# Attention scores of a hybrid decoder layer: key tiles of 288 columns, low keys on 128 rows, a PSUM bank for each query head

## The chip, the core and the metric

The kernel runs on one core of a Trainium2 chip. The time is the device time of one execution in microseconds; the comparison is between medians of several executions. TensorE (PE in the profile) multiplies matrices: a weight load (LDWEIGHTS, row PEld) puts up to 128 x 128 numbers into its array, a matmul streams the other operand through and adds into PSUM, a memory of eight banks of 512 fp32 columns for each of 128 partitions. VectorE (DVE), ScalarE (ACT) and GpSimd (POOL) do the elementwise work, SyncE (SP) issues most transfers.

## The reference

One layer of a trunk for a prompt of 2048 tokens and a sample group of 32 tokens, all in fp32. What matters here is the banded attention of the prompt:

```python
qb = q.reshape(B, nb, BLOCK, N_KV_HEADS, GROUP, HEAD_DIM)          # blocks of 128 queries
kb = jnp.concatenate([kp[:, :-1], kp[:, 1:]], axis=2)              # 256 keys: block before and own
s = jnp.einsum('bnqkgd,bnskd->bnkgqs', qb, kb) * scale
mask = (rel >= 0) & (rel < WINDOW) & (kpos[:, None, :] >= 0)
probs = sink_softmax(s, mask, sink)                                # softmax with a sink per head
o = jnp.einsum('bnkgqs,bnskd->bnqkgd', probs, vb)
```

There are 8 query heads of 64 dimensions and 2 key/value heads, so a key/value head serves four query heads. Around it stand the norms, the input projection, a convolution branch of 31 taps, the merge with two gates, the output projection and the SwiGLU.

## The kernel before

**Precision.** Weights and activations are split into a high part in fp32r and a low part (the fp32 value less the high part), and a product is three fp32r matmuls: high x high, high x low, low x high. All GEMMs are built this way, 24 matmuls for a tile of 128 outputs by one chunk of tokens.

**Stages.** The tokens form two groups: group 0 of 1024 prompt tokens in chunks of 512, group 1 of the other 1024 and the 32 sample tokens in chunks of 352. Each group goes through the input projection (`mixer_in`), the merge and output projection (`mixer_out`) and the feed-forward part (`ffn`).

**Order of work.** The program is written out by hand; each engine executes its instructions in the order in which they are issued. The GEMMs form the main stream. After each GEMM tile, `gemm_group` calls `pump`, which keeps running totals of the estimated TensorE and VectorE time (`Timed`, `pe_cost`, `dve_cost`). When a step of the attention is due (every 4200 ns of estimated TensorE time) it issues one step of `attn_gen`; then it issues convolution taps (`dw`, 1024 columns each on VectorE) as long as VectorE's total is less than 1400 ns ahead. In group 0 the units of the adaLN conditioning (`ada_unit`, tiles `wh`,`wl` by `cs`) stand between the GEMMs as well; four of them share one PSUM bank, which they hold until the result is turned.

**The attention of a block of 128 queries** takes four steps, one after each of four GEMM tiles:
- A: the probabilities of the previous block's second key/value head are transposed, the values of its first head are multiplied (`attn_pv`, PSUM tile from `mm()`, evacuated by two ScalarE copies `oa` and `ob`), then `attn_scores` for key/value head 0;
- B: the probabilities of head 0 are normalised on GpSimd, `attn_pv` for the previous block's second head, then `attn_scores` for head 1;
- C: head 1 is normalised, the block's values are transposed (`v_block`);
- D: head 0's probabilities are transposed, and the next block's keys and queries are stacked (`k_stack`, `q_stack`).

`attn_scores` is called 32 times, twice for each of 16 blocks. The stacked queries `qst` hold, for each query head, the high part on the 64 rows of its key/value head and the low part on the other 64. The high keys `kh` stand twice over the 128 rows, so one matmul of 128 rows gives (high + low query) x high key; a second one on the 64 rows of the high queries gives high query x low key. The keys are a ring of two blocks of 128 columns, 256 in all. Two query heads share a PSUM bank. VectorE then adds the mask and takes the maximum (the `CUSTOM_DVE_ANT_0` rows `p<-ps,mask`), ScalarE takes the exponentials.

**PSUM and buffers.** Of the eight banks, four belong to the GEMM pool (`mm()`), two to `ps()`, two to `pt()`. A pool gives out the bank that was freed longest ago, and the first matmul into it waits for its last reader. A bank is freed when the program drops the tile: the bank of a GEMM tile only when the next one is taken, so during an attention step the bank of the GEMM just finished is still held. Temporary tiles (`tmp`, pool `tmpp`) rotate through 13 buffers of 2 KB per partition, two of which hold `kh` and `kl` while an attention runs.

Of the kernel before, what the change touches and what calls it, by code (L numbers as in the profile page):

```python
# [10 lines left out]
F32 = mybir.dt.float32  # L11
F32R = mybir.dt.float32r
# [26 lines left out]
]  # L39
SLOT = 1056  # L40

VROWS = [("b_ada", 48), ("norm1_g", 8), ("norm2_g", 8), ("conv_b", 4), ("conv_ln_g", 4), ("conv_ln_b", 4)]
# [35 lines left out]
class Timed:  # L78
    """An engine whose instructions add their estimated length to a running total."""

# [40 lines left out]
class Builder:  # L121
    def __init__(self, ctx, tc, a, o):
        self.tc, self.nc, self.a, self.o = tc, tc.nc, a, o
        self.V = Timed(self.nc.vector, dve_cost)
        self.T = Timed(self.nc.tensor, pe_cost)
        P = bass.MemoryType.PSUM
        self.big = ctx.enter_context(tc.tile_pool(name="big", bufs=30))
        self.tmpp = ctx.enter_context(tc.tile_pool(name="tmpp", bufs=13))
        self.wrp = ctx.enter_context(tc.tile_pool(name="wrp", bufs=2))
        self.wpp = ctx.enter_context(tc.tile_pool(name="wpp", bufs=4))  # L130
        self.const = ctx.enter_context(tc.tile_pool(name="const", bufs=1))
        self.small = ctx.enter_context(tc.tile_pool(name="small", bufs=2))
        self.pmm = ctx.enter_context(tc.tile_pool(name="pmm", bufs=4, space=P))
        self.pss = ctx.enter_context(tc.tile_pool(name="pss", bufs=2, space=P))
        self.ptt = ctx.enter_context(tc.tile_pool(name="ptt", bufs=2, space=P))
        self.xT_d = [[self.dram(f"xT{g}_{f}", (128, GROUPS[g]["w"])) for f in range(KD)] for g in range(2)]
        self.gate_d = [[self.dram(f"gate{g}_{m}", (128, GROUPS[g]["w"])) for m in range(16)] for g in range(2)]
        self.tasks = []
        self.soon = []
        self.task_t = 0.0  # L140
        self.task_dt = 4200
        self.bg = []
        self.plan = []
        self.raws, self.units = [], []
# [18 lines left out]

# [1 line left out]
    def add_unit(self, key, fill):  # L165
# [169 lines left out]

# [1 line left out]
    def step(self, gens, i=0):  # L337
        """Advance a generator; None when it wants to wait for the next step."""
        try:
            return next(gens[i])  # L340
        except StopIteration:
            gens.pop(i)
            return 1

    def pump(self, slack=1400, lag=3500):
        """A step of the attention when one is due, and as much of the other side work as VectorE has time for."""
        if self.tasks and self.T.t >= self.task_t:
            self.task_t = max(self.task_t, self.T.t - 3000) + self.task_dt
            self.step(self.tasks)
        self.V.t = max(self.V.t, self.T.t - lag)  # L350
        i = 0
        while i < len(self.soon):
            if self.step(self.soon, i) is None:
                i += 1
        i = 0
        while i < len(self.bg) and self.V.t < self.T.t + slack:
            if self.step(self.bg, i) is None:
                i += 1
# [14 lines left out]

# [1 line left out]
    def gemm(self, ps, cw, terms, hi_first=False):  # L375
# [18 lines left out]
    def gemm_group(self, keys, act, g, evac, hi_first=False, ready=None):  # L394
        """GEMMs of several weight tiles, all of them on one chunk of tokens before the next chunk."""
        units = [self.w_next(k) for k in keys]
        evs = [evac(k) for k in keys]
        chunks = GROUPS[g]["chunks"]
        for n, (c0, cw) in enumerate(chunks):
            while ready is not None and ready() < c0 + cw:  # L400
                self.step(self.bg)
            for u, ev in zip(units, evs):
                ps = self.gemm_tile(u, act, c0, cw, hi_first=hi_first)
                ev(ps, c0, cw)
                self.pump()
                if n == len(chunks) - 1:
                    self.w_done()
# [11 lines left out]

# [1 line left out]
    def params_load(self):  # L421
# [49 lines left out]
    def params2(self):  # L471
# [19 lines left out]
        nc.gpsimd.memset(self.kg[:, :128], 0.0)  # L491
        self.us = c.tile([128, KC, NS], F32, name="us")
        self.vz = []
        for i in range(3):
# [57 lines left out]

# [1 line left out]
    def tok_tiles(self, g, c0, cw):  # L554
# [178 lines left out]

# [1 line left out]
    def in_evac(self, key):  # L735
        """Returns the function that takes one finished chunk of this tile of the input projection."""
        nc = self.nc
# [105 lines left out]

# [1 line left out]
    def hist_raws(self):  # L845
# [129 lines left out]
    def rstd_bcast(self, g, sm, c0, cw, ones, eps):  # L975
        """(mean over features of sm + eps) ** -0.5 for a chunk's tokens, on all partitions."""
        nc = self.nc
# [18 lines left out]

# [1 line left out]
    def vz_write(self, z, src):  # L998
        """A block's values, for kv head 0 as [hi | lo] and for kv head 1 as [lo | hi]."""
        for v in range(2):  # L1000
# [16 lines left out]
    def k_stack(self, n, bi):  # L1017
        """The keys of a block into their half of the ring: hi twice over the partitions for each kv head, lo once."""
        nc, R = self.nc, self.ROWS
        src = self.kg[:, (n + 1) * 128:(n + 2) * 128]  # L1020
        half = (bi + 1) % 2
        for kv in range(2):
            for r in range(2):
                nc.scalar.activation(out=self.kh[R[r], kv, half], in_=src[R[kv]], func=AF.Copy)
            nc.gpsimd.tensor_tensor(out=self.kl[R[kv], half], in0=src[R[kv]], in1=self.kh[R[kv], kv, half].bitcast(F32), op=ALU.subtract)

    def q_stack(self, n, kv):
        """A kv head's four query heads of a block: hi on the head's own partitions, lo on the others."""
        nc, r, o = self.nc, self.ROWS[kv], self.ROWS[1 - kv]
# [7 lines left out]
    def attn_scores(self, qs, kv, mask):  # L1037
        nc = self.nc
        r = self.ROWS[kv]
        mx = self.small.tile([128, 4], F32, tag="mx", name="mx")  # L1040
        es = self.small.tile([128, 4], F32, tag="es", name="es")
        den = self.small.tile([128, 4], F32, tag="den", name="den")
        P = []
        for jp in range(2):
            ps = self.ps()
            p = self.tmp("p")
            P += [p[:, :256], p[:, 256:]]
            for e in range(2):
                j = jp * 2 + e
                out = ps[:, e * 256:e * 256 + 256]  # L1050
                self.T.matmul(out, qs[:, j], self.kh[:, kv].rearrange("p h t -> p (h t)"), start=True, stop=False)
                self.T.matmul(out, qs[r, j], self.kl[r].rearrange("p h t -> p (h t)"), start=False, stop=True)
            for e in range(2):
                j = jp * 2 + e
                self.V.tensor_tensor_reduce(out=P[j], in0=ps[:, e * 256:e * 256 + 256], in1=mask,
                                               scale=1.0, scalar=-3e38, op0=ALU.add, op1=ALU.max, accum_out=mx[:, j:j + 1])
        sink = self.sink[:, kv * 4:kv * 4 + 4]
# [40 lines left out]
    def attn_gen(self, g):  # L1098
# [8 lines left out]
        prev = None  # L1107
        self.kh = self.tmp("kh", dt=F32R).rearrange("p (v h t) -> p v h t", v=2, h=2)
        self.kl = self.tmp("kl", 256, dt=F32R).rearrange("p (h t) -> p h t", h=2)
        self.k_stack(-1, g * 8 - 1)  # L1110
# [16 lines left out]
        for n in range(8):  # L1127
# [25 lines left out]
            yield 0  # L1153
        self.kh = self.kl = None
        pv_first()
# [105 lines left out]

# [1 line left out]
    def split(self, src, W, name, eng=None):  # L1263
# [131 lines left out]

# [1 line left out]
    def norm2(self, g):  # L1397
# [140 lines left out]
    def boot(self):  # L1538
        """From the inputs to the first four tiles of group 0's input projection, ahead of the steady stream."""
        nc = self.nc  # L1540
# [116 lines left out]

# [1 line left out]
    def program(self):  # L1659
# [59 lines left out]
```

## Time and profile before

| what | value |
| --- | --- |
| median of 3 runs | 2974.28 us (2974.13 to 2978.0) |
| span of the profiled execution | 2973.9 us, 0.4 us below the median |
| busy share PE, PEld, DVE, ACT, POOL | 96%, 85%, 48%, 30%, 37% |
| score matmuls of 128 rows | 128, mean 390 ns |
| score matmuls of 64 rows | 128, mean 412 ns |
| mask passes on VectorE | 128, mean 419 ns |

The span of the profile is the profiled execution's own time; it goes from the first to the last instruction. A row of the timeline has start, duration, engine, line, operation and tiles; the bracket at its end gives the idle time of the engine before it and what ended it. All instructions recorded through the two `Timed` engines have line 89, so groups are told apart by their tiles. Matmuls overlap in the records: the pace of a stream is read from one start to the next, not from a duration.

### The profile page before, as it was taken

How to read it: one execution, taken by the hardware profiler on the slowest of the kernel's cores; microseconds unless marked ns; L12 is line 12 of the kernel's file. 1: busy time of each engine (PE TensorE's matmuls, PEld its weight loads, DVE VectorE, ACT ScalarE, POOL GpSimd, SP SyncE). 2: the span in 40 equal slices, each digit the busy share in tenths (PEclk: the TensorE clock that was granted, in tenths of full speed). 3: DMA queues.
4: the chain of work that ended last, by engine and by line, in shares of the span. 5: the costliest groups of instructions: out<-in, count | busy, mean ns of one | idle time of the engine just before them, and what ended most of it. 6: DMA issues, size and time to landing. Idle time of an engine off the chain costs nothing. (4 is left out here: it accounts for less than half of the span.)

```text
span 2973.9 us, 37568 instructions
## 1 busy us (share of the span) xinstructions
PE 2869.8 (96%) x14852; PEld 2513.0 (85%) x14852; DVE 1426.2 (48%) x2376; ACT 894.0 (30%) x1763; POOL 1098.4 (37%) x810
## 2 busy tenths in 40 slices
PE   8998899999999999999989899999999999999998
PEld 4776677777788888888789788899999999999997
DVE  5999962363322212212669987625362222233334
ACT  4333456432211111111151455444241111111112
POOL 1467765332232232222263666322123223232223
PEclk9998999999999999999999899999999999999999
DMA  7532232442111111111242022234311111111111
GB/s 274 164 106 67 76 95 89 142 150 84 43 49 44 43 57 45 47 50 50 79 125 61 25 62 66 81 106 131 113 36 50 50 43 50 43 43 50 43 44 66
DMA packets 257110, 226.40 MB, mean 76 GB/s; under 512 B 28427, under 2 KB 218775, under 8 KB 256909
## 3 DMA queue, kind: packets, MB, share of 16 engines
q1 hardware_dynamic: 241317, 201.29, 21.7%
q10 hardware_dynamic: 15616, 22.70, 2.3%
q8 instruction: 117, 1.92, 0.3%
q14 instruction: 60, 0.49, 0.1%
HBM read 188.25 MB, written 35.81 MB: 75 GB/s over the span
## 5 line engine op out<-in xcount | busy, mean ns | idle before, releaser
L191 POOL TENSOR_TENSOR wl<-wr,wh 128x1024 fp32r<-128x1024 f32 x256 | 651.1, 2552 | 1231.6 <-ACT wh L189 1131.3
L89 PE MATMUL mm<-h2h,wh 128*128 128x352 f32 (+1 forms) x1760 | 621.4, 353 | 1.5 <-ACT h2h L673 1.5
L89 PE MATMUL mm<-h2h,wl 128*128 128x352 f32 (+1 forms) x1760 | 618.4, 351 | 0.0
L89 PE MATMUL mm<-h2l,wh 128*128 128x352 f32 (+1 forms) x1760 | 596.9, 351 | 0.8 <-DVE h2l L89 0.7
L89 DVE TENSOR_TENSOR fsg<-mm,fsg 128x352 f32<-128x352 f32 (+1 forms) x110 | 65.0, 591 | 852.7 <-PE mm L89 644.3
L89 PE MATMUL mm<-hh,wh 128*128 128x352 f32 (+1 forms) x1200 | 442.0, 369 | 21.5 <-DVE u L89 10.0
L89 DVE SCALAR_TENSOR_TENSOR x<-mm,mod_G,x 128x512 f32<-128x512 f32 (+2 forms) x480 | 307.9, 643 | 266.7 <-PE mm L89 243.3
L89 PE MATMUL mm<-hh,wl 128*128 128x352 f32 (+1 forms) x1200 | 430.1, 359 | 0.0
L89 PE MATMUL mm<-hl,wh 128*128 128x352 f32 (+1 forms) x1200 | 420.5, 359 | 1.3 <-DVE hl L89 1.3
L189 ACT ACTIVATE wh<-wr 128x1024 fp32r<-128x1024 f32 x256 | 264.5, 1050 | 487.4 <-issue 393.8
L89 DVE SCALAR_TENSOR_TENSOR dw<-u,cw,dw 128x1024 f32<-128x1024 f32 x240 | 393.4, 1653 | 4.6
L89 PEld LDWEIGHTS mm<-h2h,wh 128*128 128x128 f32 x1760 | 331.4, 188 | 35.7 <-ACT h2h L673 4.7
L89 PEld LDWEIGHTS mm<-h2h,wl 128*128 128x128 f32 x1760 | 331.4, 188 | 30.6 <-issue 0.2
L89 PEld LDWEIGHTS mm<-h2l,wh 128*128 128x128 f32 x1760 | 329.0, 188 | 33.4 <-DVE h2l L89 3.2
L89 PE MATMUL mm<-fh,wh 128*128 128x352 f32 (+1 forms) x880 | 310.0, 352 | 1.3 <-ACT fh L1444 0.8
L89 PE MATMUL mm<-fl,wh 128*128 128x352 f32 (+1 forms) x880 | 309.0, 351 | 0.6 <-POOL fl L1445 0.6
L89 PE MATMUL mm<-fh,wl 128*128 128x352 f32 (+1 forms) x880 | 308.8, 351 | 0.0
L89 PEld LDWEIGHTS mm<-hh,wh 128*128 128x128 f32 x1200 | 233.5, 195 | 54.8 <-DVE u L89 10.7
L89 PEld LDWEIGHTS mm<-hl,wh 128*128 128x128 f32 x1200 | 232.0, 195 | 23.6 <-DVE hl L89 2.2
L89 PEld LDWEIGHTS mm<-hh,wl 128*128 128x128 f32 x1200 | 232.6, 194 | 21.7
L1445 POOL TENSOR_TENSOR fl<-fsg,fh 128x352 fp32r<-128x352 f32 (+1 forms) x110 | 119.5, 1086 | 352.1 <-ACT fh L1444 352.1
L1444 ACT ACTIVATE fh<-fsg 128x352 fp32r<-128x352 f32 (+1 forms) x110 | 60.7, 551 | 424.8 <-DVE fsg L89 423.7
(272 smaller groups left out, 3797.5 us busy)
## 6 DMA issues: line engine op xcount, KB each, us to landing
wr<-in_w_ffn_in SPq DMA_DIRECT2D x88, 512.0 KB
wr<-in_w_in SPq DMA_DIRECT2D x52, 512.0 KB
wr<-in_w_ada SPq DMA_DIRECT2D x48, 512.0 KB
wr<-in_w_ffn_out SPq DMA_DIRECT2D x44, 512.0 KB
gate<-gst ACTq DMA_DIRECT2D x48, 176.0 KB
gl<-gate SPq DMA_DIRECT2D x48, 176.0 KB
xt<-in_x_prompt SPq DMA_DIRECT2D x16, 512.0 KB
gate<-gst ACTq DMA_DIRECT2D x32, 256.0 KB
```

Of the source, the lines that this page charges most:

```text
L89: return f(*args, **kw)
L189: self.nc.scalar.activation(out=hi, in_=raw, func=AF.Copy)
L191: eng.tensor_tensor(out=lo, in0=raw, in1=hi.bitcast(F32), op=ALU.subtract)
L1444: nc.scalar.activation(out=hi[:, c0:c0 + cw], in_=sg, func=AF.Copy)
L1445: nc.gpsimd.tensor_tensor(out=lo[:, c0:c0 + cw], in0=sg, in1=hi[:, c0:c0 + cw].bitcast(F32), op=ALU.subtract)
```

## The change

The ring of keys becomes two constant tiles, `kh` and `kl`, for both key/value heads, of 256 + 32 columns each, zeroed once. The low keys are kept for both heads, each on its own 64 rows beside 64 rows of zeros. Both matmuls of a head use all 128 rows of the stacked queries and all 288 columns; the columns beyond 256 are not read. Each query head gets its own PSUM bank, the first two from `ps()`, the other two from the GEMM pool, and VectorE's pass on a head is issued behind that head's two matmuls. The temporary pool has 11 buffers.

```diff
-        self.tmpp = ctx.enter_context(tc.tile_pool(name="tmpp", bufs=13))
+        self.tmpp = ctx.enter_context(tc.tile_pool(name="tmpp", bufs=11))
...
+        self.kh = c.tile([128, 2, 256 + KPAD], F32R, name="kh")
+        self.kl = c.tile([128, 2, 256 + KPAD], F32R, name="kl")
+        for t in (self.kh, self.kl):
+            nc.gpsimd.memset(t.bitcast(F32), 0.0)
...
-        half = (bi + 1) % 2
+        c0 = (bi + 1) % 2 * 128
+        s = slice(c0, c0 + 128)
         for kv in range(2):
             for r in range(2):
-                nc.scalar.activation(out=self.kh[R[r], kv, half], in_=src[R[kv]], func=AF.Copy)
-            nc.gpsimd.tensor_tensor(out=self.kl[R[kv], half], in0=src[R[kv]], in1=self.kh[R[kv], kv, half].bitcast(F32), op=ALU.subtract)
+                nc.scalar.activation(out=self.kh[R[r], kv, s], in_=src[R[kv]], func=AF.Copy)
+            nc.gpsimd.tensor_tensor(out=self.kl[R[kv], kv, s], in0=src[R[kv]], in1=self.kh[R[kv], kv, s].bitcast(F32), op=ALU.subtract)
...
-        for jp in range(2):
-            ps = self.ps()
-            p = self.tmp("p")
-            P += [p[:, :256], p[:, 256:]]
-            for e in range(2):
-                j = jp * 2 + e
-                out = ps[:, e * 256:e * 256 + 256]
-                self.T.matmul(out, qs[:, j], self.kh[:, kv].rearrange("p h t -> p (h t)"), start=True, stop=False)
-                self.T.matmul(out, qs[r, j], self.kl[r].rearrange("p h t -> p (h t)"), start=False, stop=True)
-            for e in range(2):
-                j = jp * 2 + e
-                self.V.tensor_tensor_reduce(out=P[j], in0=ps[:, e * 256:e * 256 + 256], in1=mask,
-                                               scale=1.0, scalar=-3e38, op0=ALU.add, op1=ALU.max, accum_out=mx[:, j:j + 1])
+        for j in range(4):
+            ps = self.ps() if j < 2 else self.mm()
+            if j % 2 == 0:
+                p = self.tmp("p")
+                P += [p[:, :256], p[:, 256:]]
+            for n, keys in enumerate((self.kh, self.kl)):
+                self.T.matmul(ps[:, :256 + KPAD], qs[:, j], keys[:, kv], start=(n == 0), stop=(n == 1))
+            self.V.tensor_tensor_reduce(out=P[j], in0=ps[:, :256], in1=mask,
+                                        scale=1.0, scalar=-3e38, op0=ALU.add, op1=ALU.max, accum_out=mx[:, j:j + 1])
...
-        self.kh = self.tmp("kh", dt=F32R).rearrange("p (v h t) -> p v h t", v=2, h=2)
-        self.kl = self.tmp("kl", 256, dt=F32R).rearrange("p (h t) -> p h t", h=2)
...
-        self.kh = self.kl = None
```

More of the change, by code (lines that the diff above doesn't have):

```diff
@@ L40 @@
 SLOT = 1056
+KPAD = 32
 VROWS = [("b_ada", 48), ("norm1_g", 8), ("norm2_g", 8), ("conv_b", 4), ("conv_ln_g", 4), ("conv_ln_b", 4)]
@@ L1038, in attn_scores @@
         nc = self.nc
-        r = self.ROWS[kv]
         mx = self.small.tile([128, 4], F32, tag="mx", name="mx")
```

## The prediction

> **What bounds the kernel now.** I read the page's engine shares and slices first, then a table by stage, then the order of time around one score call.
>
> ```profile
> span 2973.9 us, 37568 instructions
> PE 2869.8 (96%) x14852; PEld 2513.0 (85%) x14852; DVE 1426.2 (48%) x2376; ACT 894.0 (30%) x1763; POOL 1098.4 (37%) x810
> PE   8998899999999999999989899999999999999998
> DVE  5999962363322212212669987625362222233334
> ```
> TensorE is busy 96% of the span; VectorE is full only in slices 1 to 4 and 21 and 22 (counted from 0, 74 us each), around the beginnings of the attention and the convolution. So a saving on TensorE counts, except there, where it must be looked at stage by stage:
>
> ```profile
> 236.00:393.00 157.00, 141.45 (x584) 104.88 (x584) 143.43 (x204) 70.71 (x187) 111.77 (x99) 0.91 0.24 76
> 393.00:520.00 127.00, 127.00 (x554) 94.77 (x554) 50.70 (x159) 78.21 (x190) 72.21 (x101) 0.99 0.28 90
> 1640.00:1804.00 164.00, 146.55 (x748) 129.13 (x746) 148.82 (x245) 84.39 (x242) 110.28 (x121) 0.89 0.15 46
> 1804.00:1844.00 40.00, 39.91 (x215) 35.05 (x216) 27.22 (x72) 22.73 (x70) 25.75 (x39) 0.96 0.20 64
> 1844.00:1880.00 36.00, 31.65 (x179) 27.86 (x178) 29.46 (x74) 18.15 (x52) 19.93 (x28) 0.96 0.19 61
> ```
> Columns: length, busy PE, weight loads, DVE, ACT, POOL, then granted clock. The 16 score calls of group 0 lie in the first two stretches, those of group 1 in the last three. TensorE alone binds in the second and fourth; in the first and third it idles 16 and 17 us while VectorE is busy over 90%. One call, all engines, in order of time (start, duration, engine):
>
> ```profile
> 508.85 0.40 PE L89 MATMUL mm<-ptl,vz 128*128 128x512 f32 x1
> 508.85 0.19 PEld L89 LDWEIGHTS ps<-kh,qst 128*128 128x128 f32 x1
> 509.08 0.28 PE L89 MATMUL ps<-kh,qst 128*128 128x256 f32 x1
> 509.29 0.18 PEld L89 LDWEIGHTS ps<-kl,qst 64*128 64x128 f32 x1 [0.25 <-issue]
> 509.29 0.38 PE L89 MATMUL ps<-kl,qst 64*128 64x256 f32 x1
> 509.40 0.59 ACT L1096 ACTIVATE oa<-mm 64x512 f32<-64x512 f32 x1 [0.40 <-PE mm L89]
> 509.60 0.19 PEld L89 LDWEIGHTS ps<-kh,qst 128*128 128x128 f32 x1
> 510.01 0.59 ACT L1096 ACTIVATE ob<-mm 64x512 f32<-64x512 f32 x1
> 510.33 0.42 DVE L89 CUSTOM_DVE_ANT_0 p<-ps,mask 128x256 f32<-128x256 f32 x1 [4.59 <-PE ps L89]
> 511.17 0.38 PE L89 MATMUL ps<-kl,qst 64*128 64x256 f32 x1
> 511.48 0.50 PE L89 MATMUL mm<-hh,wh 128*128 128x512 f32 x1
> 511.81 0.40 PE L89 MATMUL mm<-hl,wh 128*128 128x512 f32 x1
> 511.94 0.42 DVE L89 CUSTOM_DVE_ANT_0 p<-ps,mask 128x256 f32<-128x256 f32 x1
> ```
> The first score load starts under the matmul before it. From the 64-row matmul on, load and matmul start together: 2.40 us for eight matmuls (509.08 to 511.48), about 0.31 each, and the first GEMM matmul after them takes 0.50 instead of 0.40, 0.10 waiting for its own load. A call costs TensorE 2.50 us. For comparison, streams of one row count:
>
> ```profile
> 900.00:1000.00 100.00, 100.00 (x435) 81.27 (x434) 20.09 (x28) 17.08 (x22) 31.43 (x16) 1.00 0.16 48
> 2300.00:2400.00 100.00, 100.00 (x621) 100.00 (x620) 26.91 (x56) 17.81 (x28) 30.97 (x19) 1.00 0.15 45
> 1933.35 0.28 PE L89 MATMUL mm<-pth,vh 128*128 128x128 f32 x1
> 1933.47 0.28 PE L89 MATMUL mm<-ptl,vh 128*128 128x128 f32 x1
> ```
> These run at 0.230 us per 512-column matmul, 0.161 per 352-column one (rows 1 and 2, length by count) and 0.11 to 0.12 at 128 columns, loads hidden.
>
> **The change, part by part.** *Row count.* All eight matmuls of a call now use 128 rows. No fp32r matmul of 288 columns is in the trace; the line through 512 and 352 gives 0.161 - 64 x 0.00043 = 0.133 us, between 0.11 (128 columns) and 0.161. I take 0.133: a call would be 8 x 0.133 = 1.06 and leave the next load covered: 1.44 saved, 46 us over 32 calls. The 32 padding columns cost 0.014 each of the eight.
>
> *Banks.* Heads 2 and 3 now take banks of the GEMM pool. The pool has four; the GEMM tile just finished is still held while the attention step is issued, and in group 0 a conditioning (adaLN) unit holds another. A freed bank is reused least recently freed first. In group 1 the order is then value product, head 2, head 3, and the next GEMM gets the value product's bank; in group 0, with two banks, head 3 gets it already, and the next GEMM gets head 2's. The value product leaves its bank by the two ACT copies: the second ends at 510.60, 1.52 after the first score matmul; before the change nothing needed that bank so soon. So in group 0 head 3 starts at about 1.57 instead of 0.80 and the call ends at 1.57 + 0.27 = 1.84, while in group 1 the next GEMM starts at about 1.6. What is left is 0.65 a call in group 0 and 0.9 in group 1. Queued behind that wait on TensorE is the next GEMM; ScalarE and VectorE get its output later by the same amount.
>
> *VectorE.* Its mask pass on a head may start after two matmuls instead of four: 509.08 to 510.33 is 1.25, new about 0.13 + 0.29 + 0.05 = 0.47. Four passes end at 512.36 now, 3.28 after the first matmul; the two middle passes then need no wait for the second pair. This shortens the softmax where VectorE was idle (4.59 us before this call).
>
> *Stage by stage.* From 393 to 520 are eight calls on a full TensorE: 8 x 0.65, less about 1 because the copies can come later, as in this call of group 1, where the second ends 2.8 us after the first score matmul: 4 us.
>
> ```profile
> 1829.24 0.28 PE L89 MATMUL ps<-kh,qst 128*128 128x256 f32 x1
> 1831.43 0.59 ACT L1096 ACTIVATE ob<-mm 64x512 f32<-64x512 f32 x1
> ```
> Before 393 TensorE waits for the query stacks of POOL, as here:
>
> ```profile
> 315.79 4.34 POOL L1034 TENSOR_TENSOR qst<-q,qst 64x128 fp32r<-64x128 f32 x8
> 317.16 0.39 PE L89 MATMUL ps<-kh,qst 128*128 128x256 f32 x1 [4.62 <-POOL qst L1034]
> 320.53 0.58 PE L89 MATMUL ps<-kl,qst 64*128 64x256 f32 x1
> 319.11 0.43 DVE L89 CUSTOM_DVE_ANT_0 p<-ps,mask 128x256 f32<-128x256 f32 x1 [1.12 <-PE ps L89]
> 321.94 0.08 DVE L89 DVE_READ_ACCUMULATOR2_ANT mx<- 128x1 f32 x1
> ```
> After such a wait the matmuls go at 0.51 (317.48 to 320.53 is 6 steps) and VectorE's last pass ends at 321.9; with heads at 0.27 and a pass per head it ends at about 319.5. I count 2 us for each of the three blocks after such waits, between 0 (the waits grow by all that is saved) and 2.4, and lose 1 in the first block (rival 5). Group 0 together: 4 + 6 - 1 = 9 us.
>
> Group 1, to 1804: ten calls, 9 us by the 0.9; I count half, 4.5, because VectorE is busy 148.8 of 164 us and POOL's stacks again end TensorE's waits; bounds 0 and 9. From 1804 to 1844: three calls, one of them that of 1829.24, so 1.5, and the call just before 1804, which waited for POOL, adds 1. The last two calls, after 1849, are hidden: the chain that ended last runs on VectorE there until
>
> ```profile
> 1873.73 2.23 DVE den L89
> 1878.41 1.54 PE ps L89 x2
> ```
> Group 1 together: 7 us.
>
> *The rest*, with three rows (a wait of the chain, a group, an instruction):
>
> ```profile
> 2055.43 3.98 DMA gl<-gate
> L1234 POOL MEMSET vh<- 128x512 f32 x4 | 2.1, 522 | 0.0
> 85.18 6.32 POOL L191 TENSOR_TENSOR wl<-wr,wh 128x1024 fp32r<-128x1024 f32 x2 [17.64 <-ACT wh L189]
> ```
> Two memsets of 576 columns on POOL cost 0.6 us each by the 522 ns and fall into the 17.64 us that POOL idles before 85.18; uncovered, 1.2. Key and query stacking keep their instructions and sizes; no DMA is added or moved. Temporary buffers go from 13 to 11, but the two key tiles that sat in them during the attention are gone, so there nothing changes; elsewhere a tile is reused two allocations sooner. Gate loads, the tightest user, are issued behind weight loads on SP's queue and their buffers' last readers are several chunks back: I take 0; the other end is one more reload wait like that of 3.98 us. The planner's matmul cost grows 0.11 us a call, which may shift a step by one GEMM: 2 us either way, taken as 0.
>
> **Sum.** 9 + 7 = 16 us. The profiled span of 2973.9 us is 0.4 below the median of the runs, 2974.28; 2974.3 - 16 = 2958 us.
>
> The Trainium skill, TensorE: Matmul & The Clock Gate, section The mechanism (Part 3), speaks against the change: it says a weight load overlaps running matmuls only when their row groups differ, so eight matmuls on the same 128 rows would load and stream in turn. The trace disagrees: 435 matmuls fit into 100 us above although each load lasts 0.19. By the rule a call would still gain, as rival 3 works out.
>
> **Rivals.** 1, *no bank waits*: the copies do not hold TensorE, the whole 1.44 counts. For: it is what the streams give. Against: the 510.01 row. 46 us less 7 in VectorE's stretch and 3 for the last two calls: 36, 2938 us. 2, *VectorE and POOL keep the rest*: only 393 to 520 and 1804 to 1844 gain, 4 + 2 us: 2968. For: over 90% VectorE there. Against: its waits for scores, as at 319.11. 3, *loads in turn*: the row at 511.48 shows 0.10 for an uncovered load, so a call is 8 x 0.236 = 1.89 in group 1, 0.61 saved, and about 2.1 in group 0, 0.4 saved; with the shares above, 60%: 9 us, 2965. The 0.230 pace speaks against. 4, *it does not do what it says*: the turn-taking has another cause than 64 rows, and eight matmuls cost 0.11 more a call: 3.5 us, 2978. 5, *slower*: in group 0 the GEMM after a call writes head 2's bank and waits for VectorE's third pass. Two rows:
>
> ```profile
> 236.06 0.28 PE L89 MATMUL ps<-kh,qst 128*128 128x256 f32 x1
> 242.90 0.42 DVE L89 CUSTOM_DVE_ANT_0 p<-ps,mask 128x256 f32<-128x256 f32 x1
> ```
> Here VectorE comes 6.8 us after TensorE and the wait would be real: the GEMM starts some 5 us later, of which the next wait for POOL's stacks (TensorE idles 16 us before 393) takes back all but the 1 us that I subtracted. A third pass ends 1.11 after the first starts, so it decides where VectorE comes later than 2.50 - 1.11 = 1.4 us. If it came at 2.4 in all 16 calls, each costs 1.0: 16 lost, 8 gained: 2982. Against: VectorE idled 4.59 us before 510.33.
>
> **How the numbers follow.** Chances: forecast 0.52 (own range 2948 to 2967), rival 1 0.20, rival 2 0.10, rival 3 0.07, rival 4 0.05, rival 5 0.06. A measurement tells 0.2%, 6 us, from no change. Faster: 0.50 of the forecast, rivals 1 and 3, half of 2: 0.82. Slower: rival 5 and a little of 4: 0.07. Same: 0.11. The range 2938 to 2970 reaches from rival 1 to rival 2 and leaves out rivals 4 and 5 and the far side of 1.
>
> **What would show it.** Score matmuls 0.13 apart with their loads started under the matmul before (right) or together with their own (rivals 3, 4); TensorE idle before head 3 in group 0, or before the GEMM matmul in group 1, released by an ACT copy (the bank waits), or by VectorE's pass (rival 5); VectorE's first pass 0.5 us after the first score matmul; longer waits for POOL's stacks (rival 2). It is wrong if the banks come free in another order than I read, or if buffers two fewer hold a transfer.

## The result and the profile after

The changed kernel takes 2957.36 us (median of 4 runs, 2956.81 to 2957.87) against 2976.14 us (4 runs, 2974.13 to 2978.64) for the kernel before beside it: a ratio of 0.9933, 95% interval 0.9919 to 0.9947, 18.8 us less. The forecast was 2958. The profiled execution took 2956.81, its span 2954.9. From the page of the changed kernel, the shares:

```profile
span 2954.9 us, 37634 instructions
PE 2826.6 (96%) x14852; PEld 2500.7 (85%) x14852; DVE 1432.5 (48%) x2376; ACT 893.6 (30%) x1763; POOL 1116.4 (38%) x812
```

TensorE is busy 43 us less than the 2869.8 of before, close to the 46 us counted as an upper limit, but the span is only 19 us shorter. Three landmarks show where: the first score matmul (236.06 us before), the transpose of `kg` with which group 1's attention begins, and the first transpose for the sample scores, after the prompt's attention. Three rows of after, then two of before, in order of time within each kernel:

```profile
233.98 0.29 PE L90 MATMUL ps<-kh,qst 128*128 128x288 f32 x1
1629.77 0.27 PE L90 MATMUL pt<-ident,kg 128*128 128x128 f32 x1
1908.41 0.38 PE L90 MATMUL pt<-ident,sc 128*128 128x128 f32 x2
```

```profile
1643.20 0.27 PE L89 MATMUL pt<-ident,kg 128*128 128x128 f32 x1
1928.14 0.38 PE L89 MATMUL pt<-ident,sc 128*128 128x128 f32 x2
```

From the first to the second landmark ("group 0" below): 1407.1 before, 1395.8 after, 11.3 less. From the second to the third ("group 1"): 284.9 and 278.6, 6.3 less. The rest: 2.1 less ahead of the first, which is scatter (a second profile of the changed kernel has 0.3), and 0.7 more behind the third. The sum is 19.0. The landmarks stand at the same place in the order of work of every kernel here, so they are used below for all.

Within group 1, busy times by stage (length, then PE, weight loads, DVE, ACT, POOL), one row of before and one of after:

```profile
1643.20:1928.00 284.80, 262.59 (x1402) 233.47 (x1401) 228.29 (x454) 139.88 (x387) 166.62 (x200) 0.92 0.19 60
```

```profile
1629.80:1908.40 278.60, 238.51 (x1406) 224.05 (x1405) 234.31 (x458) 142.19 (x390) 170.57 (x199) 0.93 0.20 61
```

TensorE was relieved of 24.1 us and the stretch became 6.2 us shorter: it now idles 40 us there instead of 22. Group 0, by contrast, has a stretch where TensorE alone binds. From its ninth score call to its sixteenth: 393.29 to 509.08 before, 115.8 us; 385.65 to 494.17 after, 108.5 us.

One of these calls, the one after `pv_second` at 463.54, all engines, rows left out where the dots stand:

```profile
463.54 0.30 PE L90 MATMUL ps<-kh,qst 128*128 128x288 f32 x1
463.54 0.19 PEld L90 LDWEIGHTS ps<-kl,qst 128*128 128x128 f32 x1
463.67 0.29 PE L90 MATMUL ps<-kl,qst 128*128 128x288 f32 x1
463.68 0.19 PEld L90 LDWEIGHTS ps<-kh,qst 128*128 128x128 f32 x1
...
464.00 0.42 DVE L90 CUSTOM_DVE_ANT_0 p<-ps,mask 128x256 f32<-128x256 f32 x1 [3.56 <-PE ps L90]
...
464.47 0.29 PE L90 MATMUL mm<-kl,qst 128*128 128x288 f32 x1
464.48 0.59 ACT L1097 ACTIVATE ob<-mm 64x512 f32<-64x512 f32 x1
...
464.70 0.42 DVE L90 CUSTOM_DVE_ANT_0 p<-mm,mask 128x256 f32<-128x256 f32 x1
...
465.18 0.50 PE L90 MATMUL mm<-hh,wh 128*128 128x512 f32 x1 [0.41 <-DVE mx L90]
```

Each load now starts with the matmul before its own. The eight matmuls start within 463.54 to 464.47, 7 steps of 0.133. VectorE's first pass comes 0.46 after the first. All four heads go through without a wait; the wait comes behind them, when the next GEMM's bank comes free: 1.64 us from the first score matmul to that GEMM instead of 2.40.

### The profile page after: what moved, and what is told of

It is laid out like the page before. It is cut to its first block, busy times and chain, and to the rows that moved or that the text cites. A ratio compares the mean times of both kernels' runs of the same rounds, so it can differ in the third digit from the quotient of the medians.

```text
span 2954.9 us, 37634 instructions
## 1 busy us (share of the span) xinstructions
PE 2826.6 (96%) x14852; PEld 2500.7 (85%) x14852; DVE 1432.5 (48%) x2376; ACT 893.6 (30%) x1763; POOL 1116.4 (38%) x812
## 5 line engine op out<-in xcount | busy, mean ns | idle before, releaser
L192 POOL TENSOR_TENSOR wl<-wr,wh 128x1024 fp32r<-128x1024 f32 x256 | 658.7, 2582 | 1205.1 <-ACT wh L190 1110.3
L90 PE MATMUL mm<-hh,wh 128*128 128x352 f32 (+1 forms) x1200 | 438.4, 365 | 33.6 <-DVE u L90 13.1
L90 PEld LDWEIGHTS mm<-hh,wh 128*128 128x128 f32 x1200 | 231.4, 193 | 66.9 <-DVE u L90 14.0
L90 PEld LDWEIGHTS mm<-hl,wh 128*128 128x128 f32 x1200 | 229.9, 193 | 22.8 <-DVE hl L90 1.7
```

The lines of the kernel that those rows point to most:

```text
L90: return f(*args, **kw)
L192: eng.tensor_tensor(out=lo, in0=raw, in1=hi.bitcast(F32), op=ALU.subtract)
```

## The experiments

"Saved" is the time against the median of the kernel before measured beside it; 95% intervals stand with the ratios, each from up to 5 runs of the kernel (11 for `e2_banks` and `e9_fixedq`). "Calls" is a sum from the trace: for each of the 32 calls the time from its first score matmul to the second matmul behind the call, waits in between included (before: 102.1 us; after: 80.2 us).

| kernel | median us | ratio, interval | saved | calls | group 0 | group 1 |
| --- | --- | --- | --- | --- | --- | --- |
| before | | | | 102.1 | 1407.1 | 284.9 |
| after | 2957.36 | 0.9933, 0.9919 to 0.9947 | 18.8 | 80.2 | 1395.8 | 278.6 |
| after_again | 2958.18 | 0.9931, 0.9918 to 0.9943 | 20.5 | 81.5 | 1395.1 | 278.7 |
| e1_rows | 2955.27 | 0.9922, 0.9910 to 0.9935 | 22.8 | 61.4 | 1395.2 | 275.5 |
| e1_again | 2956.06 | 0.9925, 0.9913 to 0.9937 | 22.6 | 61.5 | 1394.9 | 275.6 |
| e2_banks | 2982.42 | 1.0015, 1.0006 to 1.0024 | -4.4 | 115.4 | 1411.8 | 286.1 |
| e3_nopad | 2956.77 | 0.9928, 0.9916 to 0.9941 | 21.3 | 91.4 | 1398.7 | 274.1 |
| e4_grouped | 2964.89 | 0.9957, 0.9944 to 0.9969 | 13.1 | 81.8 | 1401.0 | 279.1 |
| e6_nolow | 2954.82 | 0.9918, 0.9904 to 0.9931 | 23.8 | 49.6 | 1391.5 | 275.9 |
| e7_noqlow | 2964.02 | 0.9946, 0.9933 to 0.9960 | 14.6 | 66.9 | 1393.5 | 285.4 |
| e8_tmp9 | 2993.61 | 1.0055, 1.0042 to 1.0067 | -15.4 | 69.9 | 1407.9 | 300.8 |
| e9_fixedq | 2977.57 | 0.9997, 0.9988 to 1.0006 | 0.6 | 61.2 | 1397.1 | 296.4 |
| e10_slot13 | 2953.25 | 0.9922, 0.9908 to 0.9935 | 25.2 | 58.2 | 1391.7 | 274.6 |
| e11_tmp12 | 2950.30 | 0.9907, 0.9894 to 0.9921 | 28.1 | 60.6 | 1393.3 | 273.9 |

**The row count alone.** Two heads share a bank again, both from `ps()`, with 256 columns; the low keys keep their 128 rows. The constant key tiles and the 11 buffers stay as in the changed kernel.

```diff
-        for j in range(4):
-            ps = self.ps() if j < 2 else self.mm()
...
+        for jp in range(2):
+            ps = self.ps()
...
+            for e in range(2):
...
+                self.T.matmul(out, qs[:, j], self.kh[:, kv], start=True, stop=False)
+                self.T.matmul(out, qs[:, j], self.kl[:, kv], start=False, stop=True)
```

> The changed kernel with its 128-row low keys, but 256 columns, two heads in one bank, both from ps() and the passes behind the pair, as before. My theory (the row count is the whole gain, the borrowed banks cost): score matmuls 0.12 to 0.13 us apart, a call 1.0 us instead of 2.40, no wait after the eight calls of group 0 that now wait about 0.5, and the first call of group 1 back from 17.9 us to about 8: median 2945 to 2955, faster than the changed kernel by 4 to 12 us. Rival (the banks and VectorE's earlier first pass bring the gain of the changed kernel): 2962 to 2976. Rival (the waits on banks cost nothing, since VectorE takes the time back anyway): within 2 us of the changed kernel, 2955 to 2959.

> The changed kernel once more, for a comparison on one chip with the version of two heads in one bank (e1_again). About 19 us under the kernel before, as measured (2957.36 against 2976.14). If the borrowed banks cost something in the end, e1_again is 2 to 8 us faster; if VectorE takes it back, both lie within 2 us.

> 128-row low keys, 256 columns, two heads in one bank, no bank of the GEMM pool: 20 to 25 us under the kernel before. Theory: the bank waits that it does without (0.5 us after eight calls of group 0, 9.4 us in the first call of group 1) are worth 2 to 8 us against after_again, no more, because the 9.4 fall into the stretch where VectorE is over 90% busy. Rival: nothing, within 2 us.

The row count is the whole gain: 22.8 and 22.6 us, against 18.8 and 20.5 with the separate banks. The step is 0.118 at 256 columns. From the timeline of e1_again:

```profile
495.57 0.28 PE L90 MATMUL ps<-kh,qst 128*128 128x256 f32 x1
495.57 0.19 PEld L90 LDWEIGHTS ps<-kl,qst 128*128 128x128 f32 x1
495.69 0.28 PE L90 MATMUL ps<-kl,qst 128*128 128x256 f32 x1
495.69 0.19 PEld L90 LDWEIGHTS ps<-kh,qst 128*128 128x128 f32 x1
...
496.39 0.28 PE L90 MATMUL ps<-kl,qst 128*128 128x256 f32 x1
496.40 0.19 PEld L90 LDWEIGHTS mm<-hh,wh 128*128 128x128 f32 x1
496.51 0.39 PE L90 MATMUL mm<-hh,wh 128*128 128x512 f32 x1
```

0.94 us for the call, no wait behind it, and the next GEMM's load is covered. Yet the 20 us that the calls lose against the changed kernel shorten the whole by 2.1 us where both were measured on one chip (`e1_again` and `after_again`), within the runs' scatter; the first pair, measured apart, differs by 4 us in the time saved. The rival "banks bring the gain" is gone; between about 2 us and nothing for the borrowed banks this does not decide.

**The banks alone.** The changed kernel with the low matmul on 64 rows:

```diff
-            for n, keys in enumerate((self.kh, self.kl)):
-                self.T.matmul(ps[:, :256 + KPAD], qs[:, j], keys[:, kv], start=(n == 0), stop=(n == 1))
+            self.T.matmul(ps[:, :256 + KPAD], qs[:, j], self.kh[:, kv], start=True, stop=False)
+            self.T.matmul(ps[:, :256 + KPAD], qs[r, j], self.kl[r, kv], start=False, stop=True)
```

> The changed kernel with the low matmul back on the 64 rows of the high queries: a bank for each head, 288 columns, but rows switched 64/128. My theory: matmul steps 0.31 to 0.33 again, a call 2.5 us, waits on banks smaller because the copies have come by then, the first pass 0.7 us after the first matmul: 2970 to 2982, about the kernel before. Rival (the banks bring the gain): 2955 to 2963.

It is 4.4 us slower than before; the median lies just over the range expected, and the earlier pass of VectorE buys nothing that can be seen. The row count is all that it differs in from the changed kernel, which saves 18.8 us: the row count is worth 23 us here, as much as in `e1_rows`. The constant tiles and the 11 buffers, which it has too, show no gain without it.

**The padding.**

```diff
-KPAD = 32
+KPAD = 0
```

> The changed kernel without the 32 padding columns (256 of them). If a matmul's time goes with its columns (0.133 - 32 x 0.00043 = 0.119): 256 x 0.014 = 3.5 us less work, part of it hidden: 2953 to 2956. If at 256 columns something else sets the pace (the 128-column matmuls went at 0.11 to 0.117): no change within 2 us, 2955.5 to 2959.5.

A matmul does get shorter, 0.118 for 0.133, which is 256 x 0.015 = 3.8 us. The time does not tell it from the changed kernel, so the median falls into the second range although that range's reason, an unchanged pace, does not hold. TensorE waits instead: in the stretch from 225 to 530 us it waits for VectorE's passes on the borrowed banks (row of `e3_nopad`: total, times, longest) where the changed kernel has 5.0.

```profile
PE mm L90 <- DVE mx L90: 11.7, 5, 4.3
```

**Half the changes of row count.** The kernel before, the second head of a pair with its low matmul first, so that the order is high, low, low, high:

```diff
-                self.T.matmul(out, qs[:, j], self.kh[:, kv].rearrange("p h t -> p (h t)"), start=True, stop=False)
-                self.T.matmul(out, qs[r, j], self.kl[r].rearrange("p h t -> p (h t)"), start=False, stop=True)
+                hi = lambda s, t: self.T.matmul(out, qs[:, j], self.kh[:, kv].rearrange("p h t -> p (h t)"), start=s, stop=t)
+                lo = lambda s, t: self.T.matmul(out, qs[r, j], self.kl[r].rearrange("p h t -> p (h t)"), start=s, stop=t)
+                for i, m in enumerate((lo, hi) if e else (hi, lo)):
+                    m(i == 0, i == 1)
```

> The kernel before with the order high, low, low, high in each pair of heads: the same matmuls, with half as many changes between 128 and 64 rows. If each change of row count costs (0.313 against 0.12): steps low-low and high-high 0.12 to 0.13, four or five steps of 0.31, a call 1.5 to 1.7 instead of 2.40, 2962 to 2970. If a 64-row matmul is slow by itself, whatever stands before it: a call of 2.4 still and 2974 to 2978. The high-high step would then be the only short one.

A call takes 1.72 us and the kernel 13.1 us less, as the theory of the change says. The steps of the matmuls are all 0.21 to 0.22, not short and long in turn; the loads show the pattern. Weight loads of one call (two of one row count in a row; 0.29 for two of 0.18 means that the second starts 0.11 after the first):

```profile
501.66 0.19 PEld L89 LDWEIGHTS ps<-kh,qst 128*128 128x128 f32 x1
502.10 0.29 PEld L89 LDWEIGHTS ps<-kl,qst 64*128 64x128 f32 x2 [0.25 <-issue]
502.53 0.30 PEld L89 LDWEIGHTS ps<-kh,qst 128*128 128x128 f32 x2
502.96 0.29 PEld L89 LDWEIGHTS ps<-kl,qst 64*128 64x128 f32 x2
503.39 0.19 PEld L89 LDWEIGHTS ps<-kh,qst 128*128 128x128 f32 x1
```

0.43 from pair to pair: 0.11 within it and 0.32 over a change of row count. A change costs about 0.2 us (0.21 by the loads; 0.195 by the call, whose four changes make it 1.72 instead of the 0.94 of e1), in both directions, and a 64-row matmul behind a 64-row one is as fast as a 128-row one. The Trainium skill, TensorEngine Tiling (Array Packing), section Key Properties, says that a change of tiling mode drains TensorE; this trace agrees, if 64 against 128 rows is such a change, with about 0.2 us for it.

**Less TensorE still, and less GpSimd.** Both start from e1_again. The first leaves out the matmuls with the low keys. The second leaves out the low queries, keeping the stacks in two fixed tiles and 9 temporary buffers.

```diff
-                self.T.matmul(out, qs[:, j], self.kl[:, kv], start=False, stop=True)
```

> e1_again without the high query x low key matmuls (left out of the computation): TensorE is spared a further 4 x 0.118 = 0.47 us a call, 15 us over 32 calls. Theory (of TensorE's time in a score call about half counts, that of the calls from 393 to 520 and from 1804 to 1844 us and a part elsewhere): 5 to 9 us faster than e1_again. Rival (TensorE's time counts in all calls): 13 to 16. Rival (it no longer counts): 0 to 2.

```diff
-        qs = self.tmp("qst", dt=F32R).rearrange("p (j t) -> p j t", j=4)
+        qs = self.qst[kv]
...
-            nc.gpsimd.tensor_tensor(out=qs[o, j], in0=src, in1=qs[r, j].bitcast(F32), op=ALU.subtract)
```

> e1_again without the low parts of the queries (left out of the computation: the stacked queries are two constant tiles whose low halves stay zero), so GpSimd is spared eight of ten subtractions for each block, about 0.6 us each, and TensorE's waits for the stacks (17.4 us in group 0, 15.2 in group 1 in the profile of two heads in one bank) lose their cause. Theory (VectorE, 150 of 157 and 154 of 164 us busy there, takes over as the limit): 4 to 12 us faster than e1_again, with new waits on VectorE. Rival (the stacks are the limit): 25 to 33 faster. Rival (VectorE is the limit already): 0 to 2.

`e6_nolow` misses: 12 us less in the calls give 1.2 us less, within the scatter, so TensorE's time in score calls counts little by now. Its profile has group 0 shorter by 3.4, group 1 not at all (275.9 against 275.6) and the time after the last landmark longer by 4.6. That last part lies outside the prompt's attention: in the 78.0 us behind the landmark the granted clock is 0.96, against 1.00 in the 72.9 us of the same work in e1_again, and one new wait of TensorE, for ScalarE, takes 1.1 us. `e7_noqlow` misses worse: 8 us slower with less work. The waits for GpSimd's stacks are gone from group 1, one of 6.8 us for ScalarE's part of a stack is new, and others are longer. TensorE's waits in group 1, two rows of e1_again, then two of `e7_noqlow`:

```profile
PE ps L90 <- POOL qst L1040: 15.2, 10, 3.8
PE pt L90 <- DVE vz L90: 7.0, 5, 2.1
```

```profile
PE pt L90 <- DVE vz L90: 21.6, 6, 5.3
PE ps L90 <- ACT qst L1040: 6.8, 1, 6.8
```

**Why that was slow: buffers.** First 9 temporary buffers alone, then the fixed tiles with the low queries computed again:

```diff
-        self.tmpp = ctx.enter_context(tc.tile_pool(name="tmpp", bufs=11))
+        self.tmpp = ctx.enter_context(tc.tile_pool(name="tmpp", bufs=9))
```

> e1_again with 9 temporary buffers instead of 11. The prediction put the loss of two buffers (13 to 11) at nothing. If that holds and there is room to spare, two fewer again cost under 2 us: 2954 to 2958. If buffers were already short, transfers through them and GpSimd's stacks wait longer: over 2960, and e7_noqlow, which also had 9, was slow for that reason.

```diff
-        qs = self.tmp("qst", dt=F32R).rearrange("p (j t) -> p j t", j=4)
+        qs = self.qst[kv]
```

> e7_noqlow with the low parts of the queries computed again: the stacked queries still sit in two constant tiles, with 9 temporary buffers. It tells why e7_noqlow was 8 us slower than e1_again though it does less. If the fixed tiles (a stack can't be refilled before its last score matmul) or the 9 buffers are the cause: 2960 to 2968 here too. If the missing work on GpSimd is the cause (TensorE no longer held back by it, VectorE falls behind): 2953 to 2958, like e1_again.

Two buffers fewer cost 38 us against e1_again, 13 in group 0 and 25 in group 1, nothing outside the attentions. The stage of group 1 shows no engine busier, all of them less; e1_again first, `e8_tmp9` second (columns as above):

```profile
1640.00:1905.00 265.00, 227.38 (x1339) 212.29 (x1340) 221.45 (x448) 139.10 (x386) 163.57 (x194) 0.94 0.20 62
```

```profile
1640.00:1905.00 265.00, 210.25 (x1185) 196.59 (x1184) 210.89 (x399) 130.06 (x373) 161.31 (x187) 0.89 0.15 47
```

In the same stretch two waits appear that e1_again does not have at all. VectorE's mask pass reads a `ps` bank and writes a temporary buffer `p`; in `e8_tmp9` it waits, each of the five times, for the matmuls of a value product, which read older temporary buffers (row: total, times, longest):

```profile
DVE p L90 <- PE mm L90: 20.7, 5, 7.2
```

ScalarE's copies into the stacks, temporary buffers too, wait 12.3 us, 5 times, for transposes of probabilities. Neither reads what it waits for, so these are waits for a buffer to come free. `e9_fixedq` has the first of these waits too (21.9 us), and not the second.

`e9_fixedq`, above both of its ranges, is 22 us slower than e1_again, so tiles and buffers are the cause in `e7_noqlow`, not the work left out: against `e9_fixedq` that work is worth 14 us. Which share is the fixed tiles' and which the 9 buffers' is not separated.

**More buffers.** The key tiles in a large buffer and 13 temporary ones; then 12, with room from two small tiles:

```diff
-        self.tmpp = ctx.enter_context(tc.tile_pool(name="tmpp", bufs=11))
+        self.tmpp = ctx.enter_context(tc.tile_pool(name="tmpp", bufs=13))
...
-        self.kh = c.tile([128, 2, 256 + KPAD], F32R, name="kh")
-        self.kl = c.tile([128, 2, 256 + KPAD], F32R, name="kl")
...
+        ks = self.slot("ks", 1024, F32R)
```

> e1_again with the key tiles in one large buffer of the weight and activation pool during an attention (the low half zeroed once for each group) and 13 temporary buffers, all 13 for the attention's tiles where the kernel before had 11 of them. Two buffers fewer than 11 cost 37 us (e8_tmp9). If buffers are still short at 11, two more give 5 to 15 us: 2941 to 2951, with the gain between the first score call of each group and its last, where the 37 us were lost. If 11 were enough: 2954 to 2958.

```diff
-        self.tmpp = ctx.enter_context(tc.tile_pool(name="tmpp", bufs=11))
+        self.tmpp = ctx.enter_context(tc.tile_pool(name="tmpp", bufs=12))
...
-            st = self.small.tile([NS, 128], F32, tag=name + "new", name=name + "new", bufs=1)
+            st = self.tmp(name + "new", 128)[:NS]
```

> e1_again with 12 temporary buffers (room from two small tiles of the sample attention, which now take temporary buffers). If buffers are still short at 11: about half of what 13 give or more, 2945 to 2952. If 11 were enough: 2954 to 2958.

`e11_tmp12` beats both kernels: 2950.30 (2948.70 to 2950.49), 28.1 us under the kernel before, with the row count and one buffer more. Against e1_again that is 5.5 us, inside its expected range, but measured on another chip, and the intervals of the two ratios overlap; two buffers more gave 2.6 us, less than one, and missed. The loss from 11 to 9 is far larger than any gain above 11.

## Why the prediction was right

*The matmul's pace: right.* 0.133 was forecast from the line through 512 and 352 columns, and 0.133 came. At 256 columns it is 0.118; the same line gives 0.119. Rival 3, and with it the rule of the Trainium skill that the prediction weighed (TensorE: Matmul & The Clock Gate, The mechanism, Part 3), falls on the rows at 463.54: the loads run under the matmul before.

*Which bank is waited for: wrong.* The step that failed is the claim, in the prediction and ahead of it, that the bank of the GEMM just finished is still held during the attention step. Followed through the program, it is given out as soon as its evacuation has been issued. So in group 0, from the second block on, head 3 takes that bank, which ScalarE has long emptied, and does not wait for the value product's. Of the eight calls for key/value head 1, the GEMM behind the call gets the value product's bank in four, head 2's in three, and in the first block, which has no value product, the bank of the GEMM before it. Behind the other eight calls of group 0 an adaLN unit or a small matmul comes first, and the next GEMM tile finds its bank free, except behind the very first (rival 5 below); once, at 456.10, an adaLN unit waits 0.81 us for the second copy. From the ninth call to the sixteenth, a call up to the next matmul takes 1.06 to 1.97 us, 1.50 on average, where 1.84 was forecast for all: 8 x (2.40 - 1.50) = 7.2, and this stretch gave 7.3 us instead of 4. A call of the usual kind, where the second ACT copy ends at 286.09:

```profile
285.50 0.59 ACT L1097 ACTIVATE ob<-mm 64x512 f32<-64x512 f32 x1
286.14 0.50 PE L90 MATMUL mm<-hh,wh 128*128 128x512 f32 x1 [0.35 <-ACT ob L1097]
```

In group 1 the GEMM behind the call mostly gets the bank of the GEMM before the call, and may wait for its evacuation:

```profile
1683.81 0.51 DVE L90 TENSOR_TENSOR u<-mm,sg 128x352 f32<-128x352 f32 x1
1684.37 0.43 PE L90 MATMUL mm<-hh,wh 128*128 128x352 f32 x1 [0.39 <-DVE u L90]
```

*A wait that the prediction did not have.* With two banks fewer, a late evacuation stops TensorE sooner. In the first call of group 1 VectorE stands with three of them behind convolution taps, and heads 2, 3 and the next GEMM wait for them in turn:

```profile
1649.22 0.51 DVE L90 TENSOR_TENSOR u<-mm,sg 128x352 f32<-128x352 f32 x1
...
1652.50 0.51 DVE L90 TENSOR_TENSOR u<-mm,sg 128x352 f32<-128x352 f32 x1
```

```profile
1649.88 0.58 PE L90 MATMUL mm<-kh,qst 128*128 128x288 f32 x1 [5.12 <-DVE u L90]
...
1653.16 0.58 PE L90 MATMUL mm<-kh,qst 128*128 128x288 f32 x1 [2.46 <-DVE u L90]
...
1659.16 0.63 PE L90 MATMUL mm<-hh,wh 128*128 128x352 f32 x1 [5.18 <-DVE uh L90]
```

The call takes 17.9 us where it took 8.5 before and takes 8.5 in e1_again. All of it is given back at once: from the landmark to the third call of group 1 it is 52.7 us before and 53.0 after, and e1_again, without this wait, needs 53.6.

*The sizes by group: right, partly by compensation.* Group 0 gave 11.3 for 9: 5.6 before 393 (forecast 5; by block -0.1, 0.5, 2.8 and 2.4 for -1, 2, 2 and 2) and 7.3 behind it, of which 1.5 are lost again by group 1, for a reason that I have not found. Group 1 gave 6.3 for 7. There the terms "0.9 for each of ten calls, half counted" were not what happened call by call; the half was a guess at VectorE's and GpSimd's grip, and that grip is what the runs confirm.

*Rival 1 was overrated.* It priced calls without bank waits at 2938. e1 is that case, and gave 2955 and 2956. Less TensorE time brings less and less: the first 20.3 us off the calls (`e4_grouped`) gave 13.1 us, the next 20.4 (`e1_rows`) another 9.7, and a further 12 (`e6_nolow`, against e1_again) 1.2. The waits for GpSimd's stacks grow in their place: in e1_again 17.6 us in group 0 and 15.2 in group 1, where the kernel before had these two rows from 236 to 520 and from 1640 to 1900:

```profile
PE ps L89 <- POOL qst L1034: 14.7, 4, 5.6
PE ps L89 <- POOL qst L1034: 11.9, 9, 3.5
```

The changed kernel has 11.6 and 11.7 there; its own waits on banks stand in their place. So rival 2 (VectorE and GpSimd keep the rest, 2968) was the better half of the truth: of 43 us of TensorE's work 24 came out as waits.

*Rival 4* falls with the rows at 463.54: the turn-taking came from the row counts.

*VectorE's early pass.* Its size was right (0.46 for 0.47). A gain from it does not show: e1, with the pass behind two heads, is no slower, and `e2_banks` is slower than before.

*Rival 5: it came where the prediction had counted it.* Behind the first call of group 0 the next GEMM gets head 2's bank and waits for VectorE's third pass, which ends at 240.71:

```profile
240.29 0.42 DVE L90 CUSTOM_DVE_ANT_0 p<-mm,mask 128x256 f32<-128x256 f32 x1
240.77 0.79 PE L90 MATMUL mm<-hh,wh 128*128 128x512 f32 x1 [4.19 <-DVE mx L90]
```

The next wait for GpSimd's stack gives it back (0.58 us instead of 5.59), so the first block takes 40.6 us where it took 40.5 before; the prediction had subtracted 1. Later such a GEMM waits for a third pass at 465.18 and at 495.80, at little cost: at 465.18 the pass ends at 465.12, the second ACT copy at 465.07. In `e3_nopad` three such waits, of 4.27, 3.99 and 2.38 us, are most of the 11.7 above.

*The rest, put at nothing.* The start and the end moved by 0.3 to 2.1 us either way. That taking 13 buffers to 11 is free because the attention keeps its 11 fits this, but no run has that step alone. But the other end of that term, one reload wait of 4 us, would have been far too low a price had the attention lost two: 38 us.

## What to carry to other kernels

On TensorE, matmuls that alternated between 64 and 128 rows here cost more than the zeros that make them all 128 rows; look for weight loads that start together with their own matmul. A saving on the engine that is busiest on average must be counted stage by stage: here it lost its worth as soon as GpSimd's stacks and VectorE ended the waits. Before giving up buffers or PSUM banks, follow the program through who gets each one next, and find out which stages need them: two of eleven buffers weighed twice as much as the whole change.

## What was unexpected of the hardware

The cost of a change between 64 and 128 rows is the same both ways, about 0.2 us with matmuls of 256 columns (0.32 from load to load against 0.11), and 64-row matmuls in a row are no slower than 128-row ones. A 0.19 us weight load is hidden even where matmuls start only 0.118 apart: consecutive loads then overlap each other in the records (those at 495.57 and 495.69).
